# Second pair's indices straight behind the last selection, the other pairs' behind its transposes, one PSUM bank per evacuating engine, one weight piece behind a store

## The chip, the cores and the metric

One NeuronCore of a Trainium2 chip runs the whole program in one launch. The metric is the device time of one execution in microseconds. Inputs are laid out on the host beforehand; nothing is computed there.

## The reference, cut to what matters

A decoder block over 512 tokens of width 1024, all in float32. An input projection feeds two attention branches (sparse attention with a learned indexer, and sliding-window attention), whose gated sum goes through an output projection and a layer norm. Then comes a mixture of experts, which is what this change is about:

```python
x = layer_norm(ALPHA * x + merged @ w_out, ln1_g, ln1_b)
g_sel = argmax(x @ w_group + b_group)                 # one of 4 groups
e_prob = softmax((x @ w_router + b_router)[g_sel])    # 8 experts in the group
top_p, top_i = top_k(e_prob, 2)                       # two experts per token
...
for e in range(32):
    h = silu(x @ w_gate[e]) * (x @ w_up[e])           # 1024 -> 256
    out = out + combine[:, e:e + 1] * (h @ w_down[e]) # 256 -> 1024
x = layer_norm(ALPHA * x + out, ln2_g, ln2_b)
```

Every expert's weights (3 MB) are read once, 96 MB in all.

## The kernel before, in words

Tokens lie in four blocks of 128 (NB). The experts are worked on in 16 pairs: pair w holds experts w and w + 16, each with 64 places (CAP) for tokens, so that one tile has 128 rows. A seventeenth tile ("ov", the ninth in order) takes tokens for which an expert had no place.

**Weights.** The weights come in 96 pieces of 1 MB, six to a pair: four "up" pieces (gate and up), then two "down" pieces (`pieces`, line 775). Called w0 to w95 here, pair w has w6w to w6w+5. `load_pieces(n)` issues all pieces below n that are not issued yet, on SP's DMA queue, into pages of a pool of 23 (`page`, tag "pg"). A piece whose page is still read by TensorE waits at the head of SP's queue. w0 to w17 are issued during the output projection (`PRE`, `WO_PRE`, lines 83, 84), the others in `stage(w)`, three tiles ahead.

**Output projection and routing** (lines 1049 to 1095). Sixteen units build the rows `acc[b]`. `normed(b)` (line 900) normalises a block, stores it to DRAM (`x1d`, on GpSimd's queue) and selects its experts with small VectorE operations. `queue(b)` (line 938) gives each selected token its place by a matmul (`key`). `first_gather(b)` (line 1027) gathers pair 0's tokens, already transposed, by matmuls with a 0/1 matrix into two PSUM banks `first[0]` (column chunks k = 0 to 3) and `first[1]` (k = 4 to 7): eight parts for a block.

**Indices.** `slots(i0, i1)` (line 980) builds for pairs i0 to i1-1 the 0/1 matrix G (VectorE, 128x512), multiplies it by `info` on TensorE (`collect`: token numbers, and with `weighted` the routing weights) and works out on VectorE `idx` (which rows to fetch), `wsl` (their weights) and `place` (where results go). With `weighted` false it gives only `idx` and returns a function that does the rest later. `route_weights()` (line 945) fills the weight columns of `info`.

**A pair.** `gather` (line 1110) fetches 128 rows from `x1d` by an indirect DMA on GpSimd's queue into one of two buffers. `transposed` turns them by eight TensorE transposes into two PSUM banks of four chunks each, and `evac_x` (line 1120) copies the chunks to SBUF with scale and bias. With `both`, even chunks go to ScalarE and odd ones to VectorE, so that both engines read from each bank. `up_part` is 32 matmuls of 512 columns, `hidden` the SiLU (ScalarE) and the product (VectorE), `turn_hidden` two transposes and a copy on ScalarE, `down_half` eight matmuls each. For pairs 0 to 7 (`SCATTER`) the result is scattered to DRAM by an indirect DMA; from pair 8 on it is added by further matmuls (`combine`).

**Order of work.** A planner orders the instructions of each engine by priorities and modelled times, except where an engine is kept in program order. From unit 8 on TensorE, ScalarE and VectorE are kept so (`KEEP1_E`); line 1381 ends it. GpSimd's and SP's queues are the planner's throughout. Between `queue(3)` and line 1381 the order is:

```python
run(fg, KC * NB); run(first_gather(b), KC)             # 1094, 1095
xt = {0: evac_x(first, xgs[3])}                        # 1345
weights = slots(1, 2, False)                           # 1346
... fetch(work[1]); up_part(pair 0)                    # 1371, 1373
route_weights(); weights(); slots(0, 1); slots(2, 4)   # 1375-1378
stage(work[2]); fetch(work[2]); nc.keep(False, *KEEP1_E)
```

The loop over tiles (line 1472) begins each even tile n with `slots(4 + n, 6 + n)`, then `stage`, `hidden`, the transposes of the next tile, `turn_hidden`, one eighth of the next tile's `up_part`, and the down projection. With `ahead` (the scatter pairs) the next tile's transposes stand before this tile's down projection.

Of the kernel before, what the change touches and what calls it, by code (L numbers as in the profile page):

```python
# [24 lines left out]
KC = 8  # L25
# [42 lines left out]
KEEP1_E = ('tensor', 'scalar', 'vector')  # L68
# [12 lines left out]
P_DN = 1  # L81
P_CO = 1
PRE = [3, 6]
WO_PRE = {9: 10, 10: 18}
XG_AT = 10

ORDER = ["k", "i0", "i1", "i2", "i3", "t0", "t1", "t2", "t3", "K", "b0", "g0", "b1", "g1", "b2", "g2", "b3", "g3",
# [42 lines left out]
def block_kernel(ctx: ExitStack, tc: tile.TileContext, xT, x, w_tm, w_in, w_uv, w_br, w_out, relb, oh,  # L130
                 kv_g, sinks, ln1_g, ln1_b, ln1_t, w_rt, b_rt, w_up, w_dn, ln2_g, ln2_b, out):
    nc = Engines(tc)
# [11 lines left out]
    def front_bank(tag):  # L144

        return bank("qt", 4, half["pool"]) if half["joint"] else bank(tag, 2, half["pool"])
# [4 lines left out]
    def qk_bank():  # L151
        return front_bank("qk")
# [7 lines left out]
    def page(dt, name):  # L160
        return pages.tile([P, 2048], dt, name=name, tag="pg", bufs=PAGES)
# [618 lines left out]
    def load_pieces(n, start=nc.sync.dma_start):  # L780
        for e, q in pieces[loaded["n"]:n]:
            t = page(F32, "wexp")
            if q < 2:
                start(t, w_up[e, q])
                ups.setdefault(e, []).append(t)
            else:
                start(t, w_dn[e])
                dns[e] = t
        loaded["n"] = max(n, loaded["n"])
# [110 lines left out]
    def normed(b):  # L900

        mv = small.tile([P, 2], F32, name="mv")
        rs = small.tile([P, 1], F32, name="rs")
        r = small.tile([P, 4], F32, name="rr", bufs=2)
        mx = small.tile([P, 16], F32, name="mx16", bufs=2)
        nc.vector.bn_aggr(mv, sts[b])
        nc.scalar.activation(rs, mv[:, 1:2], AF.Sqrt, bias=eps[:, 0:1])
        nc.vector.tensor_scalar(r[:, 0:1], mv[:, 0:1], -1.0, None, op0=ALU.mult)
        nc.vector.memset(mx[:, 8:16], -GONE)
        nc.vector.reciprocal(rs, rs)  # L910
        nc.vector.tensor_mul(r[:, 2:3], r[:, 0:1], rs)
        nc.scalar.activation(acc[b], acc[b], AF.Identity, scale=rs, bias=r[:, 2:3])
        store(b)
        lg = lgt[:, b]
        nc.vector.scalar_tensor_tensor(lg, cst[:, 0], r[:, 0:1], plg[:, b], op0=ALU.mult, op1=ALU.add)
        nc.vector.scalar_tensor_tensor(lg, lg, rs, cst[:, 1], op0=ALU.mult, op1=ALU.add)
        gm = tops[:, 0, b:b + 1]
        nc.vector.tensor_reduce(gm, lg[:, 0:4], axis=AX.X, op=ALU.max)
        gv = small.tile([P, 4], F32, name="gv", bufs=2)
        nc.vector.scalar_tensor_tensor(gv, lg[:, 0:4], gm, rank4, op0=ALU.is_equal, op1=ALU.mult)  # L920
        nc.vector.tensor_reduce(r[:, 1:2], gv, axis=AX.X, op=ALU.max)
        nc.vector.tensor_scalar(gv, gv, r[:, 1:2], NEG, op0=ALU.is_lt, op1=ALU.mult)
        nc.vector.tensor_tensor(lgm[:, b].rearrange("p (g e) -> p g e", g=4),
                                lg[:, 4:36].rearrange("p (g e) -> p g e", g=4),
                                gv[:, :, None].to_broadcast([P, 4, 8]), ALU.add)
        nc.vector.max(out=mx[:, 0:8], in_=lgm[:, b])
        nc.vector.tensor_copy(mx[:, 8:10], mx[:, 0:2])
        s32 = small.tile([P, NE], F32, name="s32", bufs=2)
        nc.vector.match_replace(out=s32, in_to_replace=mx[:, 8:16], in_values=lgm[:, b], imm_value=GONE)
        nc.vector.tensor_scalar(sel[:, b], s32, -2.0e38, None, op0=ALU.is_lt)  # L930
        if b == NB - 1:
            return mx
        nc.vector.tensor_copy(tops[:, 1, b:b + 1], mx[:, 0:1])

# [42 lines left out]
    idx = const.tile([P, 16], I32, name="idx")  # L977
    place = const.tile([P, 16], I32, name="place")

    def slots(i0, i1, weighted=True):  # L980

        pi = qk_bank()
        v = small.tile([P, 2, 8], F32, name="sl", bufs=4)
        c = slice(i0, i1)
        Gs = []

        def collect(a, n):
            for i, G in enumerate(Gs):
                for b in range(NB):
                    nc.tensor.matmul(pi[:, i * 8 + a:i * 8 + n], G[:, b], info[:, b, i0 + i, a:n], start=(b == 0),  # L990
                                     stop=(b == NB - 1))
            nc.vector.tensor_copy(v[:, 0:i1 - i0, a:n], pi[:, 0:16].rearrange("p (i c) -> p i c", c=8)[:, 0:i1 - i0, a:n])

        def weights():
            nc.vector.tensor_add(wsl[:, c], v[:, 0:i1 - i0, 2], v[:, 0:i1 - i0, 3])
            nc.vector.tensor_add(wsl[:, c], wsl[:, c], v[:, 0:i1 - i0, 4])
            nc.vector.scalar_tensor_tensor(v[:, 0:i1 - i0, 6], v[:, 0:i1 - i0, 5], float(T), v[:, 0:i1 - i0, 6], op0=ALU.mult, op1=ALU.add)
            nc.vector.scalar_tensor_tensor(place[:, c], tok[:, c], -1.0, v[:, 0:i1 - i0, 6], op0=ALU.add, op1=ALU.add)

        for i in range(i0, i1):  # L1000
            G = temp(BF16, "G")[:, 0:T].rearrange("p (b s) -> p b s", b=NB)
            kv = key.rearrange("p b (s e) -> p b s e", s=2)[:, :, :, i:i + 1]
            nc.vector.tensor_tensor(G.rearrange("p b (s c) -> p b s c", s=2),
                                    iot[:, None, None, 0:CAP].to_broadcast([P, NB, 2, CAP]),
                                    kv.to_broadcast([P, NB, 2, CAP]), ALU.is_equal)
            Gs.append(G)
        collect(0, 6 if weighted else 2)
        nc.vector.scalar_tensor_tensor(tok[:, c], v[:, 0:i1 - i0, 1], 128.0, v[:, 0:i1 - i0, 0], op0=ALU.mult, op1=ALU.add)
        nc.vector.tensor_scalar(v[:, 0:i1 - i0, 6], tok[:, c], 0.0, 4096.0, op0=ALU.is_equal, op1=ALU.mult)
        nc.vector.scalar_tensor_tensor(idx[:, c], tok[:, c], -1.0, v[:, 0:i1 - i0, 6], op0=ALU.add, op1=ALU.add)  # L1010
        if weighted:
            weights()
        else:
            return lambda: (collect(2, 6), weights())
# [12 lines left out]
    def first_gather(b):  # L1027

        G = places_of(0, b)

        def part(k):
            nc.tensor.matmul(first[k // 4][:, (k % 4) * P:(k % 4 + 1) * P], acc[b][:, k * P:(k + 1) * P], G,
                             start=(b == 0 and k % 4 == 0), stop=(b == NB - 1 and k % 4 == 3), skip_group_check=True)

        return [functools.partial(part, k) for k in range(KC)]

    def run(parts, n):
        for _ in range(n):
            if parts:
                parts.pop(0)()  # L1040
# [9 lines left out]
    for n, (q, b) in enumerate(units):  # L1050
# [24 lines left out]
        if n == XG_AT:  # L1075
# [3 lines left out]
            xgs = [t[:, z * D:(z + 1) * D] for t in xgs for z in range(2)]  # L1079
        if n in WO_PRE:  # L1080
            load_pieces(WO_PRE[n])

    b = NB - 1
# [8 lines left out]
    run(fg, F_C)  # L1092
    queue(b)
    run(fg, KC * NB)
    run(first_gather(b), KC)
    front.close()
    half["pool"], half["joint"] = ctx.enter_context(tc.tile_pool(name="psumb", bufs=1, space=PSUM)), True

# [21 lines left out]
    def evac_x(banks, o, both=True):  # L1120

        r = []
        for k in range(KC):
            c = o[:, k * P:(k + 1) * P]
            src = banks[k // 4][:, (k % 4) * P:(k % 4 + 1) * P]
            g, b_ = (ln1c[:, z, k:k + 1] for z in range(2))
            if both and k % 2:
                nc.vector.tensor_scalar(c, src, g, b_, op0=ALU.mult, op1=ALU.add)
            else:
                nc.scalar.activation(c, src, AF.Identity, scale=g, bias=b_)  # L1130
            r.append(c)
        return r
# [210 lines left out]


    xt = {0: evac_x(first, xgs[3])}
    weights = slots(1, 2, False)
    work = list(range(16))
    work.insert(OV_AT, "ov")
    jobs, norm2 = {}, []
# [16 lines left out]
    def fetch(w):  # L1366
        rows_of[w] = jobs[w][0]()
# [5 lines left out]
    up_part(early[0][0], xt[0], jobs[0][1], range(KC))  # L1373
    nc.vector.tensor_copy(tops[:, 1, NB - 1:NB], mx[:, 0:1])
    route_weights()
    weights()
    slots(0, 1)
    slots(2, 4)
    stage(work[2])
    fetch(work[2])  # L1380
    nc.keep(False, *KEEP1_E)
    late = []
    sums = small.tile([P, NB, 2], F32, name="sums", bufs=1)
    mv4 = small.tile([P, 4, NB + 1], F32, name="mv4", bufs=1)
# [85 lines left out]

    back, combined = {}, 0
    for n, w in enumerate(work):
        if n % 2 == 0 and 4 + n < 16:
            slots(4 + n, 6 + n)
        if n == 2:
            overflow_tiles()
# [26 lines left out]
        ahead = not last and not late  # L1503
        if ahead:
            xt[nx] = transposed(rows_of.pop(nx), 1, True)
            if n + 3 < len(work):
                fetch(work[n + 3])
        hT = turn_hidden(h, len(up))
        run(late, KC)
# [5 lines left out]
        if not last:  # L1515
            if nx not in xt:
                xt[nx] = transposed(rows_of.pop(nx), n >= PIN_N or n in PIN_S)
                if n + 3 < len(work):
                    fetch(work[n + 3])
            if w in SCATTER:  # L1520
                scattered(w, hT, dn, w_)
                late = []
            else:
                if combined == 0:
                    four_temps(F32R)
                combined += 1
                y = down_proj(hT, dn, w_)
                late = combine(places(tk_), y, then if n + 2 == len(work) else None)
# [122 lines left out]
```

## Time and profile before

| what | value |
|---|---|
| median of 3 runs | 696.54 us (696.34 to 696.59) |
| the profiled execution, its own time | 696.87 us |
| its span in the profile | 695.1 us |
| TensorE matmul busy (PE) | 654.0 us, 94% |
| VectorE busy (DVE) | 410.5 us, 59% |
| ScalarE busy (ACT) | 279.3 us, 40% |
| GpSimd busy (POOL) | 89.7 us, 13% |
| moved by DMA | 164.66 MB, 237 GB/s on average |

The span is the time between the first and the last event of the profile. All times inside it are counted from its start; the execution's own time is 1.8 us longer. The output projection ends near 405 us and the expert stage runs from there to the end. SPq is SP's queue (plain DMAs), q1 the DMA queue that it feeds, q0 the one that GpSimd feeds.

### The profile page before, as it was taken

How to read it: one execution, taken by the hardware profiler on the slowest of the kernel's cores; microseconds unless marked ns; L12 is line 12 of the kernel's file. 1: busy time of each engine (PE TensorE's matmuls, PEld its weight loads, DVE VectorE, ACT ScalarE, POOL GpSimd, SP SyncE). 2: the span in 40 equal slices, each digit the busy share in tenths (PEclk: the TensorE clock that was granted, in tenths of full speed). 3: DMA queues.
4: the chain of work that ended last, by engine and by line, in shares of the span. 5: the costliest groups of instructions: out<-in, count | busy, mean ns of one | idle time of the engine just before them, and what ended most of it. 6: DMA issues, size and time to landing. Idle time of an engine off the chain costs nothing.

```text
span 695.1 us, 9366 instructions
## 1 busy us (share of the span) xinstructions
PE 654.0 (94%) x3398; PEld 436.0 (63%) x3398; DVE 410.5 (59%) x1015; ACT 279.3 (40%) x614; POOL 89.7 (13%) x92
## 2 busy tenths in 40 slices
PE   9999998999999999999999987999998799999990
PEld 5797886766688787878799983333434344444430
DVE  5785999876455334376725656267324446555484
ACT  5663431859355544554413342212213233222360
POOL 0100000000020000003201001222222011110083
PEclk9999999999999999999999997999999999999995
DMA  8472511011581111134986586799999999999913
GB/s 318 148 254 77 195 62 60 1 62 60 182 303 61 61 61 55 68 122 160 350 329 250 198 349 261 267 417 419 422 418 419 421 417 418 417 421 421 379 51 122
DMA packets 31677, 164.66 MB, mean 237 GB/s; under 512 B 5977, under 2 KB 7265, under 8 KB 15756
## 3 DMA queue, kind: packets, MB, share of 16 engines
q1 hardware_dynamic: 22556, 144.83, 52.2%
q0 software_dynamic: 6976, 16.05, 6.4%
q10 hardware_dynamic: 2096, 3.15, 1.4%
q8 instruction: 28, 0.46, 0.3%
q14 instruction: 21, 0.17, 0.1%
HBM read 156.62 MB, written 16.29 MB: 249 GB/s over the span
## 4 chain that ended last, share of the span: by engine, by line
PE 72%; DVE 12%; DMA 11%; issue 2%; ACT 2%; POOL 1%; SPq 0%; POOLq 0%; DVEq 0%; ACTq 0%
PE mm L1106 11%; PE mm L187 9%; PE mm L189 8%; PE mm L188 8%; DMA wexp<-in_w_up_dram 6%; PE pv L1106 6%; PE mm L109 5%; PE qt L1106 5%; DVE pgS L457 3%; DVE mx L455 2%; DMA ln<-in_ln_g_dram 2%; PE pv L587 2%; DMA wraw<-in_w_in_dram 2%; DVE whl L184 1%; PE tr L669 1%
## 5 line engine op out<-in xcount | busy, mean ns | idle before, releaser
L1106 PE MATMUL mm<-wexp,xg 128*64 128x512 f32 x448 | 103.3, 600 | 2.5 <-DMA wexp<-in_w_up_dram 2.5
L187 PE MATMUL mm<-xh,whl 128*128 128x512 f32 (+1 forms) x264 | 104.7, 396 | 0.0
L188 PE MATMUL mm<-xl,whl 128*128 128x512 f32 (+1 forms) x264 | 103.4, 391 | 0.0
L189 PE MATMUL mm<-xh,whl 128*128 128x512 f32 (+1 forms) x264 | 103.3, 391 | 0.0
L1106 PEld LDWEIGHTS mm<-wexp,xg 128*64 128x64 f32 x448 | 31.5, 137 | 62.1 <-issue 53.9
L1106 PE MATMUL pv<-wexp,hT 128*64 128x512 f32 x240 | 57.2, 620 | 0.0
L187 PEld LDWEIGHTS mm<-xh,whl 128*128 128x128 f32 x264 | 50.3, 190 | 10.4 <-issue 1.8
L189 PEld LDWEIGHTS mm<-xh,whl 128*128 128x128 f32 x264 | 50.0, 190 | 10.1 <-issue 0.8
L188 PEld LDWEIGHTS mm<-xl,whl 128*128 128x128 f32 x264 | 50.0, 190 | 9.4 <-issue 1.6
L184 DVE TENSOR_TENSOR whl<-wraw,whl 128x1024 fp32r<-128x1024 f32 x34 | 41.5, 1220 | 22.5 <-ACT whl L183 20.7
L1163 DVE TENSOR_TENSOR h<-h,mm 128x256 f32<-128x256 f32 x15 | 6.3, 420 | 73.3 <-ACT h L1161 73.3
L1161 ACT ACTIVATE h<-mm 128x256 f32<-128x256 f32 x15 | 5.8, 384 | 107.7 <-PE mm L1106 100.1
L1130 ACT ACTIVATE xg<-qt,ln1c 128x128 f32<-128x128 f32 x92 | 36.4, 464 | 27.0 <-PE qt L1106 24.0
L183 ACT ACTIVATE whl<-wraw 128x1024 fp32r<-128x1024 f32 x34 | 35.7, 1054 | 15.4 <-DMA wraw<-in_w_in_dram 11.8
L1106 PEld LDWEIGHTS pv<-wexp,hT 128*64 128x64 f32 x240 | 17.3, 143 | 33.9 <-issue 30.6
L1263 DVE TENSOR_TENSOR acc<-acc,qt 128x512 f32<-128x512 f32 x56 | 34.1, 681 | 0.0
L639 DVE CUSTOM_DVE_ANT_0 La<-qk,bias 128x128 f32<-128x128 f32 (+3 forms) x32 | 15.3, 489 | 30.3 <-PE qk L638 27.7
L1106 PE MATMUL qt<-four,ct 128*128 128x512 f32 x104 | 29.0, 422 | 2.9 <-DVE four L1219 2.9
L829 POOL TENSOR_TENSOR tg<-tg 128x512 f32<-128x512 f32 x8 | 12.1, 1515 | 142.1 <-issue 122.6
L1114 POOL MEMSET xg<- 128x1024 f32 x14 | 13.3, 952 | 108.8 <-PE qt L1106 108.8
L455 DVE MAX8 mx<-pgS 128x8 f32<-128x256 f32 (+2 forms) x48 | 26.6, 555 | 0.7
L1106 PEld LDWEIGHTS qt<-four,ct 128*128 128x128 f32 x104 | 18.7, 192 | 12.9 <-issue 4.9
(362 smaller groups left out, 1350.8 us busy)
## 6 DMA issues: line engine op xcount, KB each, us to landing
wexp<-in_w_up_dram SPq DMA_DIRECT2D x64, 1024.0 KB
wexp<-in_w_dn_dram SPq DMA_DIRECT2D x32, 1024.0 KB
wraw<-in_w_in_dram SPq DMA_DIRECT2D x16, 1024.0 KB
yp<-routes POOLq DMA_DIRECT2D x8, 512.0 KB, 8.4
braw<-in_w_br_dram SPq DMA_DIRECT2D x4, 1024.0 KB
woraw<-in_w_out_dram SPq DMA_DIRECT2D x4, 1024.0 KB
back<-yp SPq DMA_DIRECT2D x4, 1024.0 KB
xraw<-in_xT_dram SPq DMA_DIRECT2D x4, 512.0 KB
```

The costliest lines, as they stand in the source:

```text
L109: i = f(*a, **k)
L183: nc.scalar.activation(hi, raw, AF.Copy)
L184: nc.vector.tensor_sub(lo, raw, hi.bitcast(F32))
L187: nc.tensor.matmul(o, a[0], b[0], start=start, stop=False)
L188: nc.tensor.matmul(o, a[0], b[1], start=False, stop=False)
L189: nc.tensor.matmul(o, a[1], b[0], start=False, stop=stop)
L455: pin(nc.vector.max(out=mx, in_=acc))
L457: pin(nc.vector.match_replace(out=acc, in_to_replace=mx, in_values=acc, imm_value=GONE))
L639: nc.vector.tensor_tensor_reduce(Ls[b], o, ta_bias[h][:, T - n:], 1.0, -3.0e38, ALU.add, ALU.max, m4[:, b:b + 1])
L1106: return lambda *a, **k: (pin if self.n else (lambda i: i))(getattr(nc.tensor, f)(*a, **k))
L1130: nc.scalar.activation(c, src, AF.Identity, scale=g, bias=b_)
L1263: nc.vector.tensor_add(a, a, pc)
```

## The change

The first piece is w17: it is no longer issued with w10 to w16 but on GpSimd's queue, in `normed` of the last block, behind the store of that block's rows.

```diff
-WO_PRE = {9: 10, 10: 18}
+WO_PRE = {9: 10, 10: 17}
+WO_LAST = 18
+F_D = 4
...
         if b == NB - 1:
+            load_pieces(WO_LAST, nc.gpsimd.dma_start)
             return mx
```

`slots` can run something between building G and the matmuls, and takes a PSUM bank for each `collect`. Pair 1's `slots` moves from behind pair 0's evacuation to behind `queue(3)`, with the first four of the last block's eight gather parts between.

```diff
-    def slots(i0, i1, weighted=True):
-
-        pi = qk_bank()
+    def slots(i0, i1, weighted=True, between=None):
...
         def collect(a, n):
+            pi = qk_bank()
...
             Gs.append(G)
+        if between is not None:
+            between()
         collect(0, 6 if weighted else 2)
...
     run(fg, KC * NB)
-    run(first_gather(b), KC)
+    parts = []
+
+    def most():
+        parts.extend(first_gather(b))
+        run(parts, F_D)
+
+    weights = slots(1, 2, False, most)
+    run(parts, KC)
```

With `both`, ScalarE evacuates the first bank (k = 0 to 3) and VectorE the second.

```diff
-            if both and k % 2:
+            if both and k >= 4:
```

The indices of the other pairs, the end of the kept order and the fetches of pairs 2 and 3 move into the first turn of the loop.

```diff
-    weights = slots(1, 2, False)
...
     route_weights()
-    weights()
-    slots(0, 1)
-    slots(2, 4)
     stage(work[2])
-    fetch(work[2])
-    nc.keep(False, *KEEP1_E)
...
-        if n % 2 == 0 and 4 + n < 16:
+        if n and n % 2 == 0 and 4 + n < 16:
             slots(4 + n, 6 + n)
...
             xt[nx] = transposed(rows_of.pop(nx), 1, True)
-            if n + 3 < len(work):
+            if n == 0:
+                nc.keep(False, *KEEP1_E)
+                weights()
+                slots(0, 1)
+            elif n + 3 < len(work):
                 fetch(work[n + 3])
...
+            if n == 0:
+                slots(2, 4)
+                fetch(work[2])
             if w in SCATTER:
                 scattered(w, hT, dn, w_)
                 late = []
+                if n == 0:
+                    fetch(work[3])
+                    slots(4, 6)
```

## Rows read from the trace of the kernel before

**Rows 1.** By stretch: busy PE, PEld, DVE, ACT, POOL; TensorE's clock, DMA share, GB/s.
```profile
413.50:416.50 3.00, 0.08 (x2) 0.03 (x2) 1.86 (x5) 2.37 (x4) 0.00 (x0) 1.00 0.96 404
...
416.50:423.50 7.00, 7.00 (x28) 2.29 (x30) 4.43 (x21) 2.18 (x5) 1.10 (x1) 0.76 0.30 67
433.50:441.50 8.00, 8.00 (x30) 2.51 (x30) 1.99 (x5) 2.04 (x5) 2.09 (x3) 0.75 0.31 76
416.50:445.00 28.50, 23.91 (x114) 9.29 (x116) 13.52 (x62) 5.22 (x12) 5.11 (x5) 0.82 0.61 225
445.00:612.70 167.70, 158.27 (x798) 65.83 (x794) 83.47 (x197) 44.51 (x105) 32.96 (x31) 0.98 1.02 418
612.70:675.00 62.30, 61.72 (x276) 27.17 (x276) 39.06 (x71) 26.80 (x58) 15.77 (x12) 1.00 0.77 319
```

**Rows 2.** Waits of TensorE, 600 to 680: us in total, times, longest.
```profile
PE mm L1106 <- DMA wexp<-in_w_up_dram: 2.5, 2, 1.4
```

**Rows 3.** The chain that ended last: start us, length us, what.
```profile
440.05 6.01 PE mm L1106 x28
...
590.74 21.89 DMA wexp<-in_w_up_dram
```

**Rows 4.** Waits of TensorE, 405 to 445.
```profile
PE qt L109 <- DVE G L109: 6.8, 4, 2.9
```

**Rows 5.** Timeline, 408 to 424: start us, us, engine, line, operation, out<-in, [idle before].
```profile
408.67 0.53 POOL L936 DMA_DIRECT2D x1d<-acc  x1 [6.06 <-ACT acc L109]
...
410.62 2.92 PE L109 MATMUL pv<-G,acc 128*128 128x128 f32 x24
...
411.05 0.29 DVE L109 TENSOR_TENSOR G<-iot,routes 128x128 f32<-128x128 f32 x1
412.69 0.46 ACT L109 ACTIVATE xg<-pv,ln1c 128x128 f32<-128x128 f32 x1 [4.31 <-PE pv L109]
413.18 0.41 DVE L109 TENSOR_SCALAR xg<-pv,ln1c 128x128 f32<-128x128 f32 x1 [1.84 <-ACT xg L109]
...
415.73 0.68 DVE L109 TENSOR_TENSOR G<-iot,routes 128x512 bf16<-128x512 f32 x1
...
416.47 0.25 PE L109 MATMUL qt<-info,G 128*128 128x2 bf16 x4 [2.92 <-DVE G L109]
...
416.65 8.78 PE L109 MATMUL mm<-wexp,xg 128*64 128x512 f32 x32
...
417.34 0.16 DVE L109 SCALAR_TENSOR_TENSOR idx<-tok,sl 128x1 int32<-128x1 f32 x1
...
418.35 1.10 POOL L1115 DMA_INDIRECT xg<-x1d,idx  x1 [9.15 <-DVE wr L109]
...
423.57 0.37 DVE L109 TENSOR_TENSOR info<-cum,wp 128x64 bf16<-128x64 f32 x1
```

**Rows 6.** Timeline of a later pair, 445 to 453.
```profile
445.99 1.09 PE L1106 MATMUL qt<-ident,xg 128*128 128x128 f32 x8
...
447.54 0.37 ACT L1183 ACTIVATE hT<-mm 128x256 f32<-128x256 f32 x1
...
452.24 6.23 PE L1106 MATMUL mm<-wexp,xg 128*64 128x512 f32 x28
```

**Rows 7.** Timeline of SP's queue, weight issues (a single issue takes 0.33).
```profile
404.57 0.33 SPq L787 DMA_DIRECT2D wexp<-in_w_dn_dram  x1
...
422.03 0.80 SPq L784 DMA_DIRECT2D wexp<-in_w_up_dram  x2
...
440.08 0.33 SPq L787 DMA_DIRECT2D wexp<-in_w_dn_dram  x1
```

**Rows 8.** Tile xg, 380 to 480: its indirect DMAs (gathers and scatters).
```profile
DMA to landing us min/median/max: 3.4/8.4/9.7
```

**Rows 9.** DMA queues, 411.9 to 416.3: packets, MB, share of 16 engines' time.
```profile
q1 hardware_dynamic: 178, 1.33, 71.4%
q0 software_dynamic: 144, 0.52, 29.1%
```

## The prediction, made before the changed kernel had run

> **What bounds the kernel now.** I read the slices first: the DMA digit is 9 from about 450 us to 660 us, the PE digit 9 almost everywhere, so two resources run full in the same stretch, and the question is which sets the end. The table by stretch gives the shares [rows 1]: from 445 to 612.7 the DMA engines are busy all the time (1.02), TensorE 158.27 of 167.7 us. The waits of TensorE then show where the two meet: from 600 to 680 it waits 2.5 us for weights [rows 2], and the chain runs through a piece that lands 21.89 us after its issue, at 612.6 [rows 3]. From 612.7 on TensorE is busy 61.72 of 62.3 us [rows 1], so whatever moves that landing moves the end by as much. Two chains lead to it. The transfer chain: the same bytes at the same full rate, so the landing moves only by idle DMA time that goes away before 445. The work chain: TensorE may come 2.5 us late against the transfers before it sets the landing's place itself. The gain is the smaller of (transfer gain) and (TensorE gain + 2.5).
>
> The idle DMA time is in the first table too [rows 1]: 28.5 us at a share of 0.61, so 28.5 x 0.39 = 11.1 us idle, in two holes: 416.5 to 423.5 (7 x 0.70 = 4.9) and 433.5 to 441.5 (8 x 0.69 = 5.5). SP's queue says why: the next weight issues come at 422.03, when half of pair 0's up projection has freed two pages, and at 440.08, when pair 0's down projection has freed the next [rows 7]. So the transfers stand still because TensorE is late with pair 0. TensorE in turn waits 6.8 us in this stretch for VectorE's matrices G [rows 4], and after each wait its granted clock is low: 0.76 and 0.75 on average in the two holes, against 0.98 from 445 to 612.7 [rows 1].
>
> **Part 1, pair 1's indices before pair 0's evacuation.** Before: the gather matmuls end at 410.62 + 2.92 = 413.54, the evacuation alternates between the two engines, G of pair 1 starts only at 415.73, and TensorE resumes at 416.47, 2.92 us idle [rows 5]. The 32 matmuls behind it take 8.78 us, where 28 take 6.01 at full clock [rows 3], so 32 would take 6.87: 1.9 us of slow clock. After: 24 records in 2.92 us are 12 parts of 0.24. Four older parts run from 410.62 to 411.6. On VectorE G (0.68) now comes ahead of the small place matrix (0.29), which moves from 411.05 to about 411.8 and ends at 412.1, so TensorE idles 0.5 us. Four parts to 413.1, the index matmuls 0.25, four parts to 414.35. ScalarE evacuates bank 0 from 413.15 in four steps of 0.46, VectorE first does the four small index steps (idx ended 417.50, 0.78 after its matmuls at 416.72; now about 414.15) and then bank 1 from 414.4 in four steps of 0.41 to 416.0 [rows 5]. TensorE can start pair 0 at 414.35 and needs a chunk every 0.43, which both engines just supply. Pair 0's up projection ends at 414.35 + 6.87 = 421.2 instead of 425.43: 4.2 us earlier. The half-second of idling I cost at no clock loss; if it did lose, 1.9 again.
>
> **Part 2, the other indices behind pair 1's transposes.** Before, 440.05 - 425.43 = 14.6 us pass between the ends of pair 0's and the start of pair 1's up projection; in a later pair it is 452.24 - 445.99 = 6.25 [rows 3, 5, 6], so 8.4 us are excess: the waits for G and a second stretch of slow clock. After, three things can still hold TensorE. (a) The routing weights: they ended 6.44 us after idx (423.94 - 417.50) [rows 5]; now they begin behind the evacuation, 416.0, and end at about 422.5. Pair 0's hidden product stands behind them on VectorE, so the transposes of the hidden cannot run before about 423. (b) Pair 1's gather. It was issued 0.85 us after idx; now at about 415.0 instead of 418.35 [rows 5]. It lands 3.4 to 9.7 us after issue [rows 8], 418.4 to 424.7; I take 422.5, since it stands behind the moved piece. Both (a) and (b) overlap, so the down projection starts near 424.6 and pair 1's up projection near 429, with some 1.5 us for five groups of index matmuls: 11 us earlier than 440.05. (c) Pair 2's gather. Its indices need, on VectorE behind pair 1's evacuation (about 425.0): pair 1's weights 0.8, pair 0's slots 0.68 + 0.78 + 0.64, two more G 1.36 and 0.78 of small steps, by the durations of [rows 5], so about 430.0; issue 430.85; landing 434.2 to 440.5, the median of 8.4 gives 439.2 [rows 8]. TensorE wants it at 429 + 6 = 435. I take a wait of 3 us (below the median, since a saturated queue carried most of those 8.4), and 1.9 of slow clock behind it. TensorE is then at pair 2's up projection at 435 + 4.9 + 6.25 = 446.1 instead of 452.24: 6.1 us earlier. Bounds: no wait, 11; both gathers at 9.7 and slow clock after each, about 1.
>
> **Part 3, the transfers.** The bytes up to 416.5 are the same, so that time stays. w19 and w20 can be issued at 414.35 + 3.4, about 418, w21 and w22 at 421.3, w23 and w24 when the down projection ends, 428 to 429. Four pieces need 10 us at 418 GB/s, so they fill 418.5 to 429 almost without a hole. I leave 3 us idle of the 11.1: one behind 416.5, one near 429, one where pair 2's wait delays the next pages. Transfer gain 8.1; bounds 0.5 and 7 us left idle: 10.6 and 4.
>
> **Part 4, the bank per engine.** In later pairs TensorE has the down projection to run while chunks 1 to 7 are evacuated, so a faster evacuation saves nothing there. It can cost: ScalarE has four steps in a row where it alternated, and the copy of the turned hidden (0.37, at 447.54 [rows 6]) may stand behind them: 0 to 0.4 us a pair, 0 to 2.8 over seven pairs, in TensorE's chain, which has 2.5 spare. I take 0.
>
> **Part 5, the piece behind the store.** w17 was issued at 404.57 [rows 7], so its page is free well before 409.2, and it does not block GpSimd. SP's next piece goes 0.4 earlier. In the 4.4 us in which the store's packets ran, GpSimd's queue got 29.1% of the engines' time and SP's 71.4% [rows 9]; with 1 MB less beside it the store ends up to 2 us sooner. The store was no limit for the gather, whose issue followed idx. The price is that pair 1's gather now stands behind 1 MB on its own queue, 2.5 us at 418 GB/s. That the queue is served in order is how I read the traces: 144 packets and exactly one block of the store in that window. The Trainium skill says the same of every ring ("DMA: Bandwidth & Descriptors", section "Queues, rings and completion order"): an engine takes descriptors in ring order and goes round the queues by packets. By that rule the gather's bytes cannot pass w17's however early idx is, and the gain of part 1 on the gather would be limited to what the emptier queue gives back; no run here shows a piece on that queue. That is the second rival below.
>
> **Sum.** The smaller of 8.1 and 6.1 + 2.5 = 8.6 is 8.1. The profiled execution took 696.87, 0.33 above the median of the runs; 696.87 - 8.1 = 688.8, in terms of the median 688.4. I say 688.5.
>
> **The rivals.** *All holes close:* both gathers land early, as the 3.4 of the lightly loaded case, and 0.5 us stays idle: gain 10.6 to 11, 685.5 to 686. Against it: the DMA engines are then full when the gathers run. *The gathers take the place of G:* pair 1's is held by w17 and pair 2's by full queues, TensorE waits 3 to 4 us before each, runs slow after each, and its pages come later; TensorE gain 2 to 3 plus 2.5, so about 5 us, 691.5. For it: 0.85 + 8.4 us from indices to landing against 6 us of up projection. *The planner's order:* behind the end of the kept order it puts index matmuls ahead of the down projection, and TensorE waits for G there as before; only part 1's 4.2 us and little of the second hole remain: about 4, 692.5, that is, most of the change would not do what it says. Against it: in the later pair the index matmuls stand behind the down projection. *Slower:* one mechanism, the gathers of pairs 1 and 2 becoming the bound on queues that are now full. The excess that goes is 4.2 + 8.4 = 12.6 and 2.5 are spare, so it decides from 15.1 us lost: waits of 3.5 and 6 us, 1.9 behind each, and the same again at pair 3, whose gather is queued behind pair 0's scatter. That gives some 17, and 698.5. Against it: pair 3 has 15 us between its indices and its need.
>
> **Chances.** Forecast 0.46 (its own range 687 to 690.5), all holes close 0.15, gathers 0.22, planner's order 0.09, slower 0.08. The range from 685.0 to 694.0 holds the first four but for their tails, about 0.83. A measurement can tell 0.2% or 1.4 us from no change: faster by more 0.87, within it 0.05 (the tails of the last two), slower 0.08.
>
> **What would show it.** Right: pair 0's up projection starts by 415 with a granted clock of 1.00 and ends near 421; SP issues w19 near 418 and w23 before 431; the DMA share from 416.5 to 445 is 0.85 or more; TensorE still waits for weights some 2 us near 600. Wrong: a wait of TensorE for xg (a gather) of over 4 us before pair 1's or pair 2's transposes, no wait for weights near 600 (then TensorE is the bound), or waits for G that stay.

## The result and the profile after

The changed kernel takes 687.62 us (median of 4 runs, 687.1 to 688.6) against 696.57 (696.34 to 697.0) for the kernel before on the same chip: a ratio of 0.9872, 95% interval 0.9855 to 0.989. The forecast was 688.5. The profiled execution took 687.62, its span is 685.5.

First the stretches of [rows 1], with the same columns. The first row is added: it covers the 11.9 us ahead of 416.5, in which the kernel before had a DMA share of 0.99. The landing that closes the full stretch is at 603, not 612.7.

```profile
404.60:416.50 11.90, 11.57 (x98) 9.51 (x98) 7.65 (x36) 5.88 (x12) 1.70 (x3) 1.00 0.97 381
416.50:423.50 7.00, 6.75 (x44) 2.86 (x40) 5.53 (x21) 3.17 (x8) 1.41 (x2) 1.00 0.77 287
...
433.50:441.50 8.00, 6.45 (x33) 2.76 (x31) 3.00 (x7) 2.16 (x6) 1.98 (x2) 1.00 1.02 397
416.50:445.00 28.50, 26.70 (x154) 10.25 (x150) 15.62 (x66) 6.71 (x16) 6.42 (x7) 1.00 0.95 374
445.00:603.00 158.00, 149.66 (x744) 62.80 (x740) 78.65 (x187) 40.10 (x98) 31.21 (x29) 0.99 1.02 419
603.00:665.00 62.00, 61.42 (x274) 27.13 (x276) 38.79 (x71) 26.55 (x57) 15.48 (x12) 1.00 0.76 316
```

The DMA share from 416.5 to 445 rose from 0.61 to 0.95: of 11.1 us idle, 28.5 x 0.05 = 1.4 are left. The clock of that stretch went from 0.82 to 1.00. Behind 445 the picture is the old one: the transfers are full up to the landing (1.02), TensorE is full behind it (61.42 of 62 us).

The waits of TensorE in the changed kernel, first from 405 to 445 (against [rows 4]), then from 585 to 680 (against [rows 2]); in us: total, times, longest.

```profile
PE qt L1118 <- DMA xg<-x1d,idx: 1.5, 1, 1.5
PE pv L111 <- DVE G L111: 0.3, 1, 0.3
PE qt L993 <- DVE info L111: 0.3, 1, 0.3
```

```profile
PE mm L1118 <- DMA wexp<-in_w_up_dram: 2.0, 2, 1.9
```

Of the 6.8 us for G 0.3 are left; in their place stands one wait of 1.5 us for pair 2's gather. The wait for weights near 600 is still there, so the transfers still set the landing. The chain that ended last (start, length, what), with the lines that answer to [rows 3]:

```profile
428.93 7.67 DMA xg<-x1d,idx
436.74 1.07 PE qt L1118 x8
...
581.00 21.92 DMA wexp<-in_w_up_dram
602.96 3.65 PE mm L1118 x14
```

The landing moved from 612.63 to 602.92, 9.7 us. The last store was issued 0.5 us earlier already (408.18 against 408.67 in [rows 5]), in a part of the program that the change doesn't touch (in all kernels of this study it lies between 408.2 and 410.0). So some 9.2 us come from the stretch between. The timeline of that stretch, with the columns of [rows 5]:

```profile
408.18 0.53 POOL L939 DMA_DIRECT2D x1d<-acc  x1 [6.06 <-ACT acc L111]
408.74 0.53 POOL L789 DMA_DIRECT2D wexp<-in_w_dn_dram  x1
...
410.55 0.89 DVE L111 TENSOR_TENSOR G<-iot,routes 128x512 bf16<-128x512 f32 x2
412.56 0.24 PE L111 MATMUL qk<-info,G 128*128 128x2 bf16 x4
412.76 1.50 ACT L111 ACTIVATE xg<-pv,ln1c 128x128 f32<-128x128 f32 x4 [4.88 <-PE pv L111]
413.41 0.16 DVE L111 SCALAR_TENSOR_TENSOR idx<-tok,sl 128x1 int32<-128x1 f32 x1
413.73 7.09 PE L111 MATMUL mm<-wexp,xg 128*64 128x512 f32 x32
413.83 1.37 DVE L111 TENSOR_SCALAR xg<-pv,ln1c 128x128 f32<-128x128 f32 x4 [0.27 <-PE pv L111]
415.86 1.10 POOL L1127 DMA_INDIRECT xg<-x1d,idx  x1 [6.59 <-DVE routes L111]
420.74 1.09 PE L111 MATMUL qt<-ident,xg 128*128 128x128 f32 x8
422.71 2.79 PE L1118 MATMUL mm<-wexp,xg 128*64 128x512 f32 x10
...
428.00 0.16 DVE L1015 SCALAR_TENSOR_TENSOR idx<-tok,sl 128x2 int32<-128x2 f32 x1
```

Pair 0's 32 matmuls run from 413.73 to 420.8 in 7.09 us, where they took 8.78; pair 1's transposes follow at once. The gather is issued 2.3 us after idx is ready (413.57), not 0.85 as before. SP's weight issues against [rows 7]:

```profile
417.40 0.80 SPq L786 DMA_DIRECT2D wexp<-in_w_up_dram  x2
...
421.26 0.39 SPq L789 DMA_DIRECT2D wexp<-in_w_dn_dram  x1
426.74 0.33 SPq L789 DMA_DIRECT2D wexp<-in_w_dn_dram  x1
430.49 1.62 SPq L786 DMA_DIRECT2D wexp<-in_w_up_dram  x3
```

The two long gaps in SP's issues, up to 422.03 and from there to 440.08, became one up to 417.40 and steps of 3.8 to 5.5 us. Last, GpSimd's queue: the landing times of the store and of w17 (KB each, us from issue to landing), then the queues from 411.6 to 415.7 (against [rows 9]), then the gathers' and scatters' landing times (against [rows 8]).

```profile
wexp<-in_w_dn_dram POOLq DMA_DIRECT2D x1, 1024.0 KB, 8.7
x1d<-acc POOLq DMA_DIRECT2D x1, 512.0 KB, 6.8
```

```profile
q0 software_dynamic: 248, 1.38, 80.2%
q1 hardware_dynamic: 48, 0.26, 20.4%
```

```profile
DMA to landing us min/median/max: 4.7/8.4/11.8
```

With w17 on its own queue behind the store, GpSimd's queue gets 80.2% of the engines where it got 29.1%. The store lands at 408.18 + 6.8 = 414.98, and the gather is issued 0.88 us later, at 415.86. So it waits for the store, not for idx. That is the one thing in this profile that the prediction excluded, and four of the experiments are about it.

### The profile page after: what moved, and what is told of

It is laid out like the page before. It is cut to its first block, busy times and chain, and to the rows that moved or that the text cites. A ratio compares the mean times of both kernels' runs of the same rounds, so it can differ in the third digit from the quotient of the medians.

```text
span 685.5 us, 9370 instructions
## 1 busy us (share of the span) xinstructions
PE 650.5 (95%) x3398; PEld 434.6 (63%) x3398; DVE 408.7 (60%) x1015; ACT 277.2 (40%) x614; POOL 90.5 (13%) x93
## 4 chain that ended last, share of the span: by engine, by line
PE 72%; DVE 12%; DMA 10%; ACT 3%; issue 2%; POOL 1%; SPq 0%; POOLq 0%; ACTq 0%; DVEq 0%
PE mm L1118 12%; PE mm L189 9%; PE mm L191 9%; PE mm L190 9%; DMA wexp<-in_w_up_dram 6%; PE pv L1118 6%; PE qt L1118 4%; PE mm L111 4%; DVE pgS L459 3%; DVE mx L457 2%; PE pv L589 2%; DMA wraw<-in_w_in_dram 2%; DVE whl L186 2%; PE tr L671 1%; DVE zb L111 1%
## 5 line engine op out<-in xcount | busy, mean ns | idle before, releaser
L1118 PE MATMUL mm<-wexp,xg 128*64 128x512 f32 x448 | 105.6, 596 | 2.0 <-DMA wexp<-in_w_up_dram 2.0
L1142 ACT ACTIVATE xg<-qt,ln1c 128x128 f32<-128x128 f32 x88 | 32.3, 464 | 20.6 <-PE qt L1118 20.4
```

Of the source, the lines that this page charges most:

```text
L1118: return lambda *a, **k: (pin if self.n else (lambda i: i))(getattr(nc.tensor, f)(*a, **k))
```

## The experiments

Times are medians of 5 to 12 runs, with a ratio to the kernel before on the same chip and its 95% interval. They were measured in three groups of four. The kernel before had medians of 696.52 (the two halves alone, the piece back on SP, the old evacuation), 694.75 (1 MB less, more work, the changed kernel again, the piece behind the gather) and 696.46 (the rest). Its single runs spread from 693.8 to 698.5, so the comparisons within a group count more than the ratio. Of the three groups only the second holds a measurement of the changed kernel; comparisons with it from the others use its two medians, 687.62 and 687.69. Differences of 1 us between medians are at the edge of what these runs tell apart.

**The first half alone.** Everything but pair 1's earlier indices is put back.

```diff
-WO_PRE = {9: 10, 10: 17}
+WO_PRE = {9: 10, 10: 18}
...
-            if both and k >= 4:
+            if both and k % 2:
...
+    weights()
+    slots(0, 1)
+    slots(2, 4)
     stage(work[2])
+    fetch(work[2])
...
```

> Only pair 1's indices move (behind the last selection, with four gather parts between); the other pairs' indices, the alternating evacuation and the piece on SP stay as before. Theory A (idle DMA time before 445 us is what the change removes, and the end follows the transfers): pair 0's up projection ends some 3.5 to 4.2 us earlier, the first hole of the transfers shrinks by that, the second hole stays near 5.5 us; gain 3 to 4.5 us, 692 to 693.6. Rival B (the end follows TensorE's own time, wherever it is saved): 4.2 us saved on TensorE plus the shorter wait later, also 4 to 5 us, but with the DMA idle time of the second hole it would not matter whether it closed. Rival C (the early indices alone are the whole gain): 687.6 to 689.

Measured 694.07 (693.17 to 695.16), ratio 0.9973 (0.9963 to 0.9983). The first two waits of TensorE from 405 to 445, and the stretches from 416.5 to 445, of this kernel:

```profile
PE qt L111 <- DVE G L111: 3.8, 3, 2.0
PE qt L111 <- DVE info L111: 2.3, 1, 2.3
...
```

```profile
416.50:423.50 7.00, 4.74 (x26) 1.46 (x22) 3.99 (x16) 2.57 (x5) 1.10 (x1) 1.00 0.73 260
433.50:441.50 8.00, 8.00 (x40) 2.67 (x38) 0.75 (x1) 0.69 (x1) 1.29 (x2) 1.00 0.63 208
416.50:445.00 28.50, 21.69 (x120) 9.20 (x118) 14.53 (x61) 7.59 (x18) 6.37 (x7) 0.88 0.74 275
```

The first hole shrinks from 4.9 us to 7 x 0.27 = 1.9. Behind it TensorE still waits for G of the later pairs, and idle time stays: 28.5 x 0.26 = 7.4 us in all, where it was 11.1. The gain is 2.5 us in the median and 3.7 in the profiled execution (693.17); theory A had given 3 to 4.5, so the median lies short of it.

**The other half alone.** Pair 1's indices go back behind pair 0's evacuation, with the old evacuation and w17 on SP.

```diff
-    weights = slots(1, 2, False, most)
-    run(parts, KC)
+    run(first_gather(b), KC)
...
     xt = {0: evac_x(first, xgs[3])}
+    weights = slots(1, 2, False)
```

> Only the indices of the other pairs and the fetches of pairs 2 and 3 move into the loop's first turn; pair 1's indices stay behind pair 0's evacuation, with the alternating evacuation and the piece on SP. Theory A: the first hole (4.9 us idle) stays, the second (5.5 us) shrinks to 1 to 2; gain 3.5 to 5 us, 691.6 to 693. TensorE by itself would save up to 8.4 us here, so rival B (the end follows TensorE) gives 688 to 690. Rival C (the early indices are the whole gain): 696 to 696.6.

Measured 691.03 (688.67 to 692.39), ratio 0.9926 (0.9904 to 0.9947). Its stretches from 416.5: the first hole is where it was, with its slow clock, and what follows it is full.

```profile
416.50:423.50 7.00, 7.00 (x30) 2.24 (x30) 4.49 (x22) 2.08 (x5) 1.10 (x1) 0.76 0.25 59
423.50:433.50 10.00, 10.00 (x64) 3.91 (x62) 6.97 (x32) 3.05 (x7) 1.49 (x2) 1.00 0.99 414
```

The halves gain 2.5 and 5.5 us, the whole change 8.9. Theory A's 691.6 to 693 was a little too slow. The first half works mainly on the first hole, the second half on the second.

**What bounds: 1 MB less.** One weight piece of pair 5 is not loaded (its expert's down weights are those of expert 5), beside a second measurement of the changed kernel: 687.69 (686.39 to 688.7), ratio 0.9882 (0.986 to 0.9904).

> The changed kernel once more, as the mark for the three runs beside it: 687.6, 687.1 to 688.6.

```diff
+            if (e, q) == (21, 2):
+                dns[e] = dns[5]
+                continue
```

> The changed kernel without one of the 96 weight pieces (the down weights of expert 21 are not loaded, expert 5's are used in their place): 1 MB, 2.4 us of transfer time, less ahead of the landing near 603 us, TensorE's work unchanged. Theory A (the end follows the transfers up to that landing, with TensorE 2.0 us ahead of them): 1.5 to 2.4 us faster than the changed kernel, 685.2 to 686.1, and the wait for weights near 600 goes. Rival B (the end follows TensorE's own chain): no change, 687.6.

Measured 685.84 (685.03 to 688.66), ratio 0.9867 (0.9843 to 0.9891), 1.85 us less than the changed kernel. TensorE's waits from 585 to 680 no longer hold one for weights:

```profile
PE qt L111 <- ACT hT L111: 0.4, 1, 0.4
PE mm L111 <- DVE h L111: 0.2, 1, 0.2
```

Five of its six runs lie at or below 686.61, nine of the ten runs of the changed kernel above 686.8. So the transfers set the landing: 1 MB is 2.5 us at 419 GB/s, 1.85 come through, then TensorE is the bound. How much TensorE has to spare differs between executions: its wait for weights there was 2.0 us in the first profile of the changed kernel and 0.9 in the second.

**What bounds: more work.** Three more halves of a down projection in pair 5, whose results nobody reads, 5.2 us of TensorE.

```diff
+        for _ in range(3 if w == 5 else 0):
+            down_half(hT, dn, 0)
```

> The changed kernel with three more half down projections in pair 5, their results unused: 24 matmul records, 5.2 us of TensorE time near 475 us, no transfer added. Theory A with the 2.0 us that TensorE waits for weights later as slack: 5.2 - 2.0 = 3.2 us slower, 690.4 to 691.4, and no wait for weights near 600. Rival B (no slack, the end follows TensorE): 5.2 slower, 692.8. Rival H (the transfers alone count): unchanged.

Measured 691.38 (689.77 to 694.44), ratio 0.9941 (0.992 to 0.9962), 3.7 us more than the changed kernel. In the profile the added matmuls take 5.15 us and no wait for weights is left between 585 and 680. By the medians TensorE had some 1.5 us to spare; the rest of the added work came through. With the run before, the rule of the smaller of two gains is shown from both sides.

**The piece back on SP's queue.** Only w17 moves back, the rest of the change stays.

```diff
-WO_PRE = {9: 10, 10: 17}
+WO_PRE = {9: 10, 10: 18}
```

> The changed kernel with w17 back on SP's queue. Theory A: the same bytes by 416.5 us; the block's store shares its time with SP's pieces again and lands 2 to 3 us later, so pair 1's gather is issued near 417.2 instead of 415.86 but has no piece ahead of it on its queue and lands within a microsecond of where it did: 687.3 to 688.4. Rival F (the piece ahead of the gather costs): 686 to 687. Rival G (the store landing late holds pair 1's gather and TensorE with it, 2 us and a spell of slow clock): 689 to 691.

Measured 693.92 (693.16 to 695.68), ratio 0.9975 (0.9961 to 0.999): 6.3 us of the gain gone with one line, where my theory gave 687.3 to 688.4 and rival G, which has the mechanism, 689 to 691. Its waits, its timeline, and the store's landing:

```profile
PE qt L111 <- DMA xg<-x1d,idx: 5.5, 1, 5.5
```

```profile
417.57 1.10 POOL L1127 DMA_INDIRECT xg<-x1d,idx  x1 [8.46 <-DMA x1d<-acc]
417.81 3.76 SPq L786 DMA_DIRECT2D wexp<-in_w_up_dram  x3
426.67 1.94 PE L111 MATMUL qt<-ident,xg 128*128 128x128 f32 x8 [5.45 <-DMA xg<-x1d,idx]
```

```profile
x1d<-acc POOLq DMA_DIRECT2D x1, 512.0 KB, 8.1
```

The transposes start at 426.67, 5.9 us later than in the changed kernel (420.74). Part comes from the issue: the store, issued at 408.57, shares the engines with w17 and lands after 8.1 us, at 416.67, and the gather follows 0.9 later, 1.71 after the changed kernel's. The larger part is the gather itself: 9.1 us from its issue to the transposes, where it landed after 4.7. It is issued 0.24 us before SP's next pieces, and its packets run only from 422 to 426, beside them. Set side by side, gather 1 of the kernels measured (its issue; the next weight issue of SP; the distance; from issue to landing, or to the last packet or the transposes where the landing isn't given; us):

```
                           gather   SP       distance   to landing
the other half alone       418.25   421.93   3.7        4.3
bank rule in pair 0 only   416.00   417.68   1.7        4.4
the changed kernel         415.86   417.40   1.5        4.7
both pieces moved          416.57   417.50   0.9        6.5
the first half alone       417.25   417.60   0.35       some 8.5 (last packet before 426)
piece back on SP           417.57   417.81   0.24       9.1 (transposes)
```

The nearer SP's refill, the later the gather: two kernels that issue it before 417.6 have it in only at about 426 and 426.7, the one that issues it at 418.25 into idle queues at 422.55. Four more kernels whose landing the trace gives (the changed kernel again, more work, the bank rule alone, the piece alone) have distances of 1.6 to 5.0 us, and the gather lands after 4.4 to 4.7 us. So from 1.5 us on the distance no longer matters.

The packets' start times in the traces say more. Where the queues stand empty (the other half alone, the piece alone), the gather's first packet runs 1.7 us after its issue; SP's first new packet runs 0.95 us after its own. In the two slow kernels SP's packets are therefore first on the engines, 1.3 and 1.2 us after the gather's issue, and the gather's first packet runs only 4.5 and 4.8 us after it. With both pieces moved the gather's first packet comes at 1.7 us, SP's 0.2 us behind it, and the gather then shares the engines. In these kernels the delay goes with whose packets come first. Why a gather that comes second stands still for three more microseconds is not shown by these traces. It also fits that the parts don't add up: the other half alone, with later indices, takes 691.03; pair 1's early indices and the bank rule added to it, without the piece, make 693.92, as the gather then goes out just ahead of SP's refill.

**The piece behind the gather.** w17 stays on GpSimd's queue but is issued behind gather 1.

```diff
-            load_pieces(WO_LAST, nc.gpsimd.dma_start)
...
+    with tc.issue_after(gathers[0].ins):
+        load_pieces(WO_LAST, nc.gpsimd.dma_start)
```

> The changed kernel with w17 on GpSimd's queue behind pair 1's gather instead of ahead of it. Piece on SP had cost 6.3 us: the store landed later, the gather was issued at 417.57 instead of 415.86, its packets ran only from 422 on beside SP's next pieces, and TensorE waited 5.5 us. Theory S (what counts is that the store has the engines to itself, so that the gather runs before SP's next pieces): the gather is issued at 414.4 to 415 and lands before 420, no wait of TensorE for it; 686.8 to 688.3. Rival Q (the piece directly ahead on the same queue is what keeps the gather's turn): the gather's packets start late again and TensorE waits some us; 690 to 694.

Measured 689.59 (688.27 to 693.22), ratio 0.9922 (0.9895 to 0.9949), 1.9 us more than the changed kernel. The gather is issued at 415.83, as in the changed kernel, and TensorE waits for neither kernel's gather 1. The time lies between the two theories' ranges. Standing behind 1 MB cost the gather nothing that the end sees, so rival Q's mechanism is out. Theory S had no term for what is lost, which lies in the stretch before:

```profile
404.60:416.50 11.90, 11.57 (x99) 9.51 (x99) 7.68 (x36) 5.88 (x12) 1.20 (x2) 1.00 0.75 297
```

The share is 0.75 where the changed kernel has 0.97: w17 fills 11.9 x 0.22 = 2.6 us that otherwise stand empty between the store and SP's refill.

**Two pieces there.** w16 moves to GpSimd's queue too.

```diff
-WO_PRE = {9: 10, 10: 17}
+WO_PRE = {9: 10, 10: 16}
```

> The changed kernel with w16 and w17 on GpSimd's queue behind the last store. Theory A: the bytes up to 416.5 are the same, the store has still less beside it, the gather may be issued up to 1 us earlier but has 2 MB ahead of it and starts when they are through, near 416.5 as before: 687.0 to 688.2. Rival K (the earlier store brings the gather and all behind it forward): 686 to 686.8. Rival L (the gather, late behind two pieces, meets SP's next pieces): 689 to 694.

Measured 693.25 (690.09 to 695.21), ratio 0.9972 (0.9958 to 0.9986): 5.6 us worse than with one piece. In its waits TensorE stands for gather 1:

```profile
PE qt L111 <- DMA xg<-x1d,idx: 2.3, 1, 2.3
```

The store lands after 7.4 us, the gather is issued at 416.57 and lands 6.5 later. But w16 does not stand where the expectation has it. GpSimd's queue is in the planner's order, and the planner put w16 ahead of the last store:

```profile
402.22 0.53 POOL L789 DMA_DIRECT2D wexp<-in_w_dn_dram  x1
408.27 0.53 POOL L939 DMA_DIRECT2D x1d<-acc  x1 [5.53 <-ACT acc L111]
```

So the store stands behind 1 MB on its own queue, and lands 0.6 us later after its issue than in the changed kernel (6.8). Two pieces behind the store were not tried, and none of the three theories is tested by this run as it was meant; what it adds is a gather issued 0.9 us ahead of SP's refill. Besides, the execution profiled is the fastest of its runs, 690.09; why the others take some 3 us more stays open.

**The piece alone**, in the kernel before.

```diff
-WO_PRE = {9: 10, 10: 18}
+WO_PRE = {9: 10, 10: 17}
+WO_LAST = 18
...
+            load_pieces(WO_LAST, nc.gpsimd.dma_start)
```

> The kernel before with only w17 moved behind the last store on GpSimd's queue. In the changed kernel this move is worth 6.3 us. Theory A: before, pair 1's gather waits for its indices (417.5), not for the store, and is wanted only at 431; so nothing is gained or lost: 696.2 to 696.9. Rival I (the store's early landing is worth the same by itself): 690 to 692. Rival J (a piece on GpSimd's queue costs by itself): 698 or more.

Measured 696.58 (694.89 to 699.08), ratio 1.0007 (0.9993 to 1.0022): nothing. Its store lands after 6.5 us, its gather is issued at 418.62 behind idx. The same edit is worth nothing where the indices are late and 6.3 us where they are early.

**The old evacuation in the changed kernel.**

```diff
-            if both and k >= 4:
+            if both and k % 2:
```

> The changed kernel with the alternating evacuation put back for all pairs. Theory A: pair 0's up projection waits up to 1 us more for its chunks (VectorE comes to chunk 1 only after the index steps), nothing in later pairs reaches the end: 687.6 to 688.6. Rival D (a bank per engine saves time in each scatter pair): 689 to 691. Rival E (it costs time in each scatter pair, by the turned hidden behind four copies on ScalarE, and that reaches the end): 685.5 to 687.

Measured 688.74 (688.53 to 692.13), ratio 0.9907 (0.9885 to 0.9929), 1.1 us more than the changed kernel. Pair 0's evacuation in its timeline, then TensorE's wait for the routing weights:

```profile
414.17 0.81 ACT L111 ACTIVATE xg<-pv,ln1c 128x128 f32<-128x128 f32 x2 [0.71 <-DVE xg L111]
414.66 0.76 DVE L111 TENSOR_SCALAR xg<-pv,ln1c 128x128 f32<-128x128 f32 x2 [0.53 <-ACT xg L111]
...
415.95 0.41 DVE L111 TENSOR_SCALAR xg<-pv,ln1c 128x128 f32<-128x128 f32 x1 [0.53 <-ACT xg L111]
```

```profile
PE qt L993 <- DVE info L111: 2.2, 1, 2.2
```

The two engines take turns, each idle until the other's chunk is done, and VectorE's last chunk ends at 416.36; with a bank each, they run side by side and it ends at 415.20. The routing weights, which are worked out behind it, come later too, and TensorE waits 2.2 us for them ahead of pair 0's down projection, where it waited 0.3.

**The bank rule alone**, in the kernel before (the same line turned the other way).

> The kernel before with only the evacuation changed (a bank per engine). So far every kernel's time is 685.8 us plus the DMA idle time between 404.6 and 445 us, within 0.4. Theory A: pair 0's evacuation ends 0.6 to 0.8 us earlier and so does all behind it; the idle time shrinks by as much: 695.7 to 696.0. Rival D (worth more, in each pair): 694 to 695. Rival E (costs in each scatter pair): 697 or more.

Measured 696.6 (693.33 to 697.24), ratio 0.9994 (0.9979 to 1.001): nothing that can be measured, where theory A had given 0.6 to 0.8 us. TensorE's wait for G does shrink, from 6.8 us:

```profile
PE qt L109 <- DVE G L109: 5.9, 4, 2.1
```

**The bank rule in pair 0 only**, the other pairs alternating.

```diff
+        first_one = banks is first
...
-            if both and k >= 4:
+            if both and (k >= 4 if first_one else k % 2):
```

> The changed kernel with a bank per engine for pair 0 only and alternating evacuation for later pairs. Theory A: in later pairs nothing of it reaches the end while TensorE waits for weights near 600: 687.2 to 688.0. Rival E (the four copies in a row on ScalarE cost 0.1 to 0.4 us a pair and that reaches the end): 685.5 to 686.8. Rival D (the bank per engine helps every pair): 688.5 or more.

Measured 687.79 (686.88 to 688.82), ratio 0.989 (0.9868 to 0.9911): the changed kernel's time. Its waits near 600:

```profile
PE mm L1118 <- DMA wexp<-in_w_up_dram: 2.9, 3, 1.4
```

What the rule gains lies in pair 0. Whether it costs TensorE anything in the other pairs is not shown: the wait of 2.9 us stands against 2.0 and 0.9 in the two profiles of the changed kernel, which differ by as much between themselves. The end sees no such cost.

**All of them on one line.** With idle = 11.9 x (1 - share of 404.6 to 416.5) + 28.5 x (1 - share of 416.5 to 445), in the profiled executions:

```
                            shares        idle   685.8 + idle   measured
before                      0.99  0.61    11.2   697.0          696.87
piece alone                 0.99  0.59    11.8   697.6          698.01
bank rule alone             0.99  0.66     9.8   695.6          697.15
piece back on SP            0.98  0.73     7.9   693.7          694.0
first half alone            0.97  0.74     7.8   693.6          693.17
other half alone            0.99  0.81     5.5   691.3          691.11
piece behind gather         0.75  0.96     4.1   689.9          689.5
two pieces                  0.97  0.87     4.1   689.9          690.09
old evacuation              0.98  0.91     2.8   688.6          688.53
changed, again              0.98  0.93     2.2   688.0          687.77
bank rule in pair 0 only    0.98  0.94     1.9   687.7          687.18
changed                     0.97  0.95     1.8   687.6          687.62
```

The 685.8 is fitted, and was on record before the last four kernels were measured (bank rule alone, piece alone, two pieces, bank rule in pair 0 only). The slope of one is not fitted; a free fit of both to the eleven without the bank rule alone gives a slope of 1.04. Eleven of twelve lie within 0.6 us. The bank rule alone is off by 1.5: there the last store was issued at 410.00, 1.3 us later than in the kernel before, which fits an execution that was late ahead of both windows. Left out are the two kernels in which the bytes or the work behind 445 differ (1 MB less, more work). These are single executions: with two pieces the one profiled lies 3 us below its median, and the line says nothing of the others.

## Why the prediction was right, point by point

**The bound** was right and is shown: the landing near 612 moves by the idle DMA time that goes away, as long as TensorE gains that less its slack. The slack was taken as 2.5 us; the two runs on it give 1.5 to 1.9, the waits in the two profiles of the changed kernel 2.0 and 0.9.

**Part 1** was right in TensorE: pair 0's up projection begins at 413.73 (forecast 414.35) and ends at 420.8 (421.2) at a full clock. It was wrong in the gather's reason: the issue at 415.0 was to follow idx; it came at 415.86, behind the store, though idx was ready at 413.57.

**Part 2** was right in direction, and its size was off: TensorE is at pair 2's transposes at 436.74, 9.25 us earlier, where 6.1 was forecast (439.9). Two terms: the planner put 14 of pair 1's up matmuls ahead of pair 0's down projection, so that up projection began at 422.71, not 429, and idx of pair 2 came at 428.16 instead of 430.0; and the wait for gather 2 was 1.5 us, not 3, with a clock of 1.00 behind it. Its 7.67 us to landing lie inside the bounds of [rows 8]. The rival of the planner's order fell, but not because the order stayed: the planner did put two groups of index matmuls ahead of pair 0's down projection (at 425.43 and 426.63), and TensorE waited for no G there.

**Part 3** was right: w19 and w20 went out from 417.40 on (forecast 418), w22 at 421.26 (421.3), w23 and w24 at 426.74 and 430.49 (428 to 429). 1.4 us of idle time were left, not 3. That is most of the difference between the forecast and the result (688.5 against 687.62): the landing came 9.7 us earlier instead of 8.1, of which 0.5 was there before the change began to act.

**Part 4** cost nothing in the later pairs, as said. But pair 0 was left out of the account: there the chunks of one bank, taken in turns, push back the routing weights. With the rest of the change the rule is worth some 1.1 us, and a rule for pair 0 only gives the changed kernel's time; without the rest, nothing that can be measured.

**Part 5** failed. "The store was no limit for the gather, whose issue followed idx" was read from a kernel in which idx was late; part 1 itself made it early, and the store became the limit. The store also landed only 1.3 us sooner after its issue (6.8 against 8.1 with the piece on SP), not up to 2. The piece was entered as a price; it is worth 6.3 us. The second rival, gathers that take the place of G, at 691.5, was one line away: with the piece on SP the kernel takes 693.92. That I met the time in spite of it is luck: the change contained the cure for a limit that I had not seen.

On the order within a queue: in the changed kernel GpSimd's queue moves w17 up to 416.6 and the gather's packets from 417.5 on. The Trainium skill says that an engine takes descriptors in ring order ("DMA: Bandwidth & Descriptors", section "Queues, rings and completion order"). This trace agrees, but does not test it: issued at 415.86, the gather would send its first packet near 417.5 even with nothing ahead of it. That is also why the price of 2.5 us did not come. w17 was through before the gather's first packet could run; with the piece behind the gather, the gather is issued at the same time and TensorE waits for neither.

## What to carry to other kernels

When a change makes something early, list everything that its consumer waits for again, and date each: a wait that was hidden becomes the bound. Here it was the store, which landed 1.4 us after the early idx (414.98 against 413.57). A small transfer that an engine waits for should be issued well ahead of a refill of bulk transfers, or be counted at twice its time: here it took 4.3 to 4.7 us when SP's next issue was 1.5 us or more away, and 8.5 to 9.1 when it was under 0.4 away. Where a bulk queue is full from some point on, the idle time ahead of that point is the time to be had, one for one, as long as the compute engine keeps up.

## What was not expected of the hardware

The delay of an indirect DMA depended on how soon another queue was refilled, by a factor of two, though that refill came after its own issue: with nothing in the way, SP's first packet runs 0.95 us after its issue, the gather's 1.7 us after its own.

And TensorE's clock stayed at 1.00 behind a wait of 1.5 us (the row of 433.5 to 441.5), while with the piece on SP, in the stretch of the wait of 5.5 us and behind it, it was 0.66 on average:

```profile
423.50:433.50 10.00, 6.83 (x36) 3.54 (x36) 4.12 (x20) 1.89 (x5) 0.95 (x1) 0.66 0.67 281
```

The length of the wait alone does not decide it. Behind waits of 2.3 and 2.2 us for pair 2's gather (1 MB less, the piece behind the gather) the clock of the row of 433.5 to 441.5 is 1.00. Behind the wait of 2.3 us for gather 1 with two pieces moved, the eight transposes take 1.94 us instead of 1.09, and the clock of 423.5 to 433.5 is 0.85. What makes the difference is not shown.
